# The low parts of the projection weights: formed on VectorE in place of GpSimd, with the steps of two recurrent branches ordered anew

## The chip, the cores and the metric

The kernel runs on one core of a Trainium2 chip. The metric is device time in microseconds (us) for one execution; of several runs the median counts. The engines are written as in the profile: PE is TensorE's matmul, PEld its weight load, DVE is VectorE, ACT is ScalarE, POOL is GpSimd, SP is SyncE, which issues most DMAs.

## The reference

One layer works on 512 tokens of width 1024 in float32. Cut to what matters here:

```python
h = _rmsnorm(x, norm1[l])
proj = h @ w_in[l]                      # 1024 -> 10256 columns
a_q, a_k, a_v, a_beta, a_alpha, a_gate, b_f, b_i, b_q, b_gate, g_a, g_b = _split_cols(proj)
...                                     # causal conv + silu on a_q, a_k, a_v
o_a = _gated_delta_rule(qa, ka, va, beta, log_alpha)        # 8 heads of 128
...
o_b = _hgrn2_recurrence(qb, 1.0 - f_gate, ib, jnp.log(f_gate))   # 8 heads of 128
y_a = ... @ w_branch_a[l];  y_b = ... @ w_branch_b[l]
x = x + (sigmoid(g_a) * y_a + sigmoid(g_b) * y_b) @ w_out[l]
x = x + _peer(_rmsnorm(x, norm2[l]), w_pq[l], ...)          # expert retrieval
return _rmsnorm(x, final_norm)
```

## The kernel before

**Weights come in units.** A unit is 128 columns of a weight matrix, held as 128 partitions x 1024 float32 (512 KB). The first 64 units of the projection are eight for each head (a_k, a_q, b_q, a_v, b_f, b_i, b_gate, a_gate); the gate units g_a and g_b are mixed in. `NPROJ` is 78: units 0 to 77 are worked off in the projection stage, which is the subject here; 78 and 79, then the branch matrices and all that follows belong to later stages.

**Each product is made of three.** `w_split` (L482) splits a unit: ACT copies `wraw` into `whi`, a rounded fp32r copy, and another engine forms the low part `wlo` = `wraw` - `whi` (L491). The activations h are split the same way into `hhi` and `hlo`. For each of eight slices of 128 rows `piece` (L503) issues three 128x512 matmuls: whi on hhi, wlo on hhi, whi on hlo; so a unit is 24 matmuls.

**Three buffers each.** The tiles wraw, whi and wlo have three buffers. When unit n begins, the projections load unit n+3 (`w_raw`, an SP DMA) and split unit n+2 (`w_cut`), so a split is due two units ahead of its use.

**The start.** For units 0 to 4 the matmuls run on unscaled h; meanwhile the token scales are found (ACT squares, DVE adds them into `acc`, PE sums across partitions, POOL takes the power, DVE spreads the scale into `rd`, PE broadcasts it). Then DVE scales these units' results and convolves a_k and a_q (L943, L947), then makes the scaled h slice by slice (L451) and splits it anew (`hlo`, L456, even slices on DVE, odd ones on POOL). Unit 5 needs that new split. `w_cut(2)` to `w_cut(6)` stand by hand between these steps.

**The rest of the stage is ordered by a planner.** Five generators run side by side: the set-up of gates and masks, branch A's state recurrence (`branch_a2`), branch A's preparation (`branch_a1`), branch B, and the projections. Each yields the tiles that its next step on PE reads. A class `Flow` keeps a model of every engine with a cost for every instruction and for the waits between engines. At each turn the loop takes the generator whose next step is ready first by that model, with small advantages (`BIAS`), and issues it. All engines then run their instructions strictly in the order in which they were issued. So a changed engine in one helper changes the costs, and with them the order of the steps on every engine. Branch A has a loop of 15 steps on POOL for each head (`xt`, `Xb`, L712 and L714) that inverts 16x16 blocks; its result goes out and back by DMA (L716 to L726) to `branch_a2`.

Of the kernel before, what the change touches and what calls it, by code (L numbers as in the profile page):

```python
# [51 lines left out]
NPROJ = 64 + 14  # L52
# [19 lines left out]
NDMA = 4  # L72
# [205 lines left out]
def build(ctx, tc, I, O):  # L278
# [6 lines left out]
    def act(o, i, f, **kw):  # L285
        nc.scalar.activation(o, i, f, **kw)  # L286

    vec, gps, pe = nc.vector, nc.gpsimd, nc.tensor
# [180 lines left out]
    N0 = len(order)  # L469
# [5 lines left out]
    raws, wts = {}, {}  # L475
# [6 lines left out]
    def w_split(raw, eng=gps):  # L482
        hi = wpool.tile([P, DC, UW], F32R, tag="whi", name="whi")
        lo = wpool.tile([P, DC, UW], F32R, tag="wlo", name="wlo")
        act(hi, raw, AF.Copy)
        if eng is None:

            act(lo, hi.bitcast(F32), AF.Copy, scale=-1.0)
            gps.dma_start(out=lo, in_=raw, accum_op=OP.add)
        else:  # L490
            eng.tensor_tensor(lo, raw, hi.bitcast(F32), OP.subtract)  # L491
        return hi, lo
# [5 lines left out]

    def w_cut(n):
        if n < len(order):  # L500
            wts[n] = w_split(raws.pop(n), vec if n < 2 else gps if n < N0 + NDMA else None)

    def piece(p, w, c, m):  # L503
        whi, wlo = w
# [8 lines left out]
    with ExitStack() as ph:  # L513
# [476 lines left out]
        def projections():  # L990
            def some():
                while late:
                    if next(late[0], True) is None:
                        return
                    late.pop(0)

            for n, (kind, h) in list(enumerate(order[:NPROJ]))[NF:]:
                while not allowed(kind, h):
                    some()
                    yield [None]  # L1000
                p = pst("mm", MMB)
                yield [wts[n][0], wts[n][1], p]
                w_raw(n + 3)
                w_cut(n + WB - 1)
                for c in range(DC):
                    piece(p, wts[n], c, hm)
                    some()
                    if n < NF + NTWO:
                        some()
                    if c < DC - 1:  # L1010
                        yield []
                wts.pop(n)
                late.append(consume(kind, h, p))
                if n >= NPROJ - 1:
                    while late:
                        some()
# [16 lines left out]
        for c in range(DC):  # L1033
            if c in (0, 2):
                cs = slice(2 * c, 2 * c + 4)
                act(wts[0][0][:, cs, :], raw[:, cs, :], AF.Copy)
                vec.tensor_tensor(wts[0][1][:, cs, :], raw[:, cs, :], wts[0][0][:, cs, :].bitcast(F32), OP.subtract)
            unscaled(xT, n1, c)
            piece(first[0], wts[0], c, hm)
            if c == W1:  # L1040
                w_cut(1)
        w_cut(2)
        w_raw(3)
        sums = pst("mA", 1)
        r = pst("mC", 1)
        rs = sbt("tmpB", 3)
        for k in range((NF - 1) * DC):
            n, c = 1 + k // DC, k % DC
# [566 lines left out]
    with ExitStack() as ph:  # L1615
# [132 lines left out]
        for i in range(-LEAD, P):  # L1748
            n = i + LEAD
# [66 lines left out]
```

## Time and profile before

| what | value |
|---|---|
| time, median of 3 runs (lowest, highest) | 2110.07 us (2106.29, 2113.62) |
| the profiled execution's own time | 2111.22 us |
| its span, first to last instruction | 2109.3 us |
| mean granted TensorE clock | 0.993 |
| busy in the span: PE, PEld, DVE, ACT, POOL | 97%, 83%, 69%, 44%, 55% |
| the stage under study | from the start to about 660 us of the span |

The shares are means over stages of very different kind; the second half of the program has DMA engines busy at 80% and more, the projection stage at 27%. What this change is worth has to be read in the first 660 us. A busy PE is a sum of modelled durations: matmuls overlap, so its share alone doesn't say that PE is at its rate.

### The profile page before, as it was taken

Reading aid. Unit: us, or ns where it says so; the run is one execution under the profiler, and the core shown is the slowest. Engines: PE = TensorE matmul, PEld = TensorE weight load, DVE = VectorE, ACT = ScalarE, POOL = GpSimd, SP = SyncE. Lnnn points to the kernel's source line nnn. Section 1 sums busy time; section 2 is a strip of 40 time slices with the busy share of each in tenths; the row PEclk is TensorE's granted clock in tenths of the full one; section 3 lists DMA queues with packets and bytes.
Section 4 is the critical chain, followed back from the end, with each engine's and each line's share of the span. In section 5 each row is a group of like instructions: output and inputs, shape, how many; then the busy total and the mean of one; then the engine's idle time right before and its main releaser. Section 6 shows DMA issues by size and latency. Waiting matters only on the chain. (4 is left out here: it accounts for less than half of the span.)

```text
span 2109.3 us, 34910 instructions
## 1 busy us (share of the span) xinstructions
PE 2039.1 (97%) x13210; PEld 1751.5 (83%) x13210; DVE 1450.8 (69%) x2779; ACT 936.4 (44%) x1742; POOL 1155.1 (55%) x957
## 2 busy tenths in 40 slices
PE   7899999999999999999899999999999999999997
PEld 5688787887878888888778999999999999999776
DVE  7666546656661375999995666676666667666897
ACT  5555555555554323666675333333333333333233
POOL 3565646654644644211002666676666666666887
PEclk9999999999999999999999999999999999999999
DMA  3322222132322644688799898988889888888785
GB/s 132 117 82 77 69 90 72 62 98 62 98 67 97 205 145 155 173 203 196 221 333 323 307 320 284 317 294 307 300 297 315 290 305 306 306 299 286 245 266 211
DMA packets 189463, 439.44 MB, mean 208 GB/s; under 512 B 26960, under 2 KB 90608, under 8 KB 187632
## 3 DMA queue, kind: packets, MB, share of 16 engines
q1 hardware_dynamic: 95248, 230.75, 32.2%
q0 software_dynamic: 42912, 156.26, 23.7%
q10 hardware_dynamic: 51136, 50.22, 7.2%
q8 instruction: 103, 1.69, 0.3%
q14 instruction: 64, 0.52, 0.1%
HBM read 375.81 MB, written 39.34 MB: 197 GB/s over the span
## 5 line engine op out<-in xcount | busy, mean ns | idle before, releaser
L491 POOL TENSOR_TENSOR wlo<-wraw,whi 128x1024 fp32r<-128x1024 f32 x204 | 501.1, 2457 | 290.5 <-ACT whi L286 283.1
L283 PE MATMUL h<-hhi,wlo 128*128 128x384 f32 x1024 | 347.0, 339 | 8.3 <-DMA wlo<-wraw 8.3
L283 PE MATMUL h<-hhi,whi 128*128 128x384 f32 x1024 | 347.7, 340 | 2.0 <-ACT hext L286 2.0
L283 PE MATMUL h<-hlo,whi 128*128 128x384 f32 x1024 | 346.7, 339 | 1.5 <-POOL hlo L456 1.1
L283 PE MATMUL mm<-hhi,whi 128*128 128x512 f32 x792 | 328.8, 415 | 1.0 <-ACT a_k L286 0.6
L283 PE MATMUL mm<-hlo,whi 128*128 128x512 f32 x792 | 311.5, 393 | 4.2 <-POOL hlo L456 3.0
L1707 DVE TENSOR_TENSOR wl<-hg,wh 128x384 fp32r<-128x384 f32 x126 | 129.4, 1027 | 269.5 <-ACT wh L286 269.5
L283 PE MATMUL mm<-hhi,wlo 128*128 128x512 f32 x792 | 309.6, 391 | 0.7 <-POOL wlo L491 0.7
L286 ACT ACTIVATE whi<-wraw 128x1024 fp32r<-128x1024 f32 (+1 forms) x251 | 263.6, 1050 | 103.1 <-PE mm L283 46.2
L283 PE MATMUL y<-vh,wl 128*128 128x512 f32 x756 | 298.7, 395 | 0.6 <-DVE wl L1707 0.6
L283 PE MATMUL y<-vl,wh 128*128 128x512 f32 x756 | 297.1, 393 | 0.9 <-POOL vl L1708 0.9
L283 PE MATMUL y<-vh,wh 128*128 128x512 f32 x756 | 295.1, 390 | 2.5 <-ACT wh L286 2.5
L1630 POOL DMA_INDIRECT row<-eu,eidx x128 | 158.3, 1236 | 145.9 <-DVE stage L1636 131.0
L1630 POOL DMA_INDIRECT row<-ev,eidx x128 | 160.9, 1257 | 126.5 <-DVE stage L1644 101.5
L286 ACT ACTIVATE hext<-h 128x384 f32<-128x384 f32 x88 | 43.1, 490 | 375.6 <-PE h L283 374.4
L283 PEld LDWEIGHTS h<-hhi,wlo 128*128 128x128 f32 x1024 | 193.7, 189 | 13.5 <-DMA wlo<-wraw 9.5
L283 PEld LDWEIGHTS h<-hhi,whi 128*128 128x128 f32 x1024 | 193.8, 189 | 6.6 <-ACT hext L286 2.6
L283 PEld LDWEIGHTS h<-hlo,whi 128*128 128x128 f32 x1024 | 193.7, 189 | 2.4 <-POOL hlo L456 1.8
L1644 DVE SCALAR_TENSOR_TENSOR stage<-row,stage 128x1024 f32<-128x1024 f32 x127 | 192.7, 1517 | 0.6
L1636 DVE CUSTOM_DVE_ANT_0 stage<-row,h2g 128x1024 f32<-128x1024 f32 x128 | 183.1, 1431 | 0.7
L283 PEld LDWEIGHTS mm<-hlo,whi 128*128 128x128 f32 x792 | 148.6, 188 | 40.1 <-POOL hlo L456 4.7
L283 PEld LDWEIGHTS mm<-hhi,whi 128*128 128x128 f32 x792 | 149.0, 188 | 27.6 <-ACT a_k L286 1.0
(431 smaller groups left out, 3675.2 us busy)
## 6 DMA issues: line engine op xcount, KB each, us to landing
wraw<-eut SPq DMA_DIRECT2D x128, 512.0 KB, 4.5
stage<-ev SPq DMA_DIRECT2D x126, 512.0 KB, 4.9
wraw<-wu SPq DMA_DIRECT2D x119, 512.0 KB, 4.1
stage<-gD ACTq DMA_DIRECT2D x31, 768.0 KB, 10.1
gD<-stage ACTq DMA_DIRECT2D x11, 2048.0 KB, 9.2
wlo<-wraw POOLq DMA_DIRECT2D x42, 512.0 KB, 5.7
sg<-sgD SPq DMA_DIRECT2D x16, 256.0 KB, 2.7
sgD<-tmpP SPq DMA_DIRECT2D x14, 256.0 KB, 2.1
```

The source lines that it names most:

```text
L283: nc.tensor.matmul(o, l, r, start=start, stop=stop)
L286: nc.scalar.activation(o, i, f, **kw)
L491: eng.tensor_tensor(lo, raw, hi.bitcast(F32), OP.subtract)
L1630: gps.indirect_dma_start(out=r, out_offset=None, in_=I["eu" if k < P else "ev"], in_offset=bass.IndirectOffsetOnAxis(ap=eidx[:, kk:kk + 1] ...
L1636: vec.tensor_tensor_reduce(out=junk, in0=r, in1=h2g, scale=1.0, scalar=0.0, op0=OP.mult, op1=OP.add, accum_out=hd[:, k:k + 1])
L1644: vec.scalar_tensor_tensor(yg, r, wgt[:, k - P:k - P + 1], yg, OP.mult, OP.add)
L1707: vec.tensor_tensor(wl, hg, wh.bitcast(F32), OP.subtract)
```

## The change

One expression differs. The engine that forms wlo is DVE for all units below 78, where it was DVE for units 0 and 1 only:

```diff
     def w_cut(n):
         if n < len(order):
-            wts[n] = w_split(raws.pop(n), vec if n < 2 else gps if n < N0 + NDMA else None)
+            wts[n] = w_split(raws.pop(n), vec if n < NPROJ else gps if n < N0 + NDMA else None)
```

So 76 subtractions of 128x1024 (units 2 to 77) go from POOL to DVE. The planner meets other costs and orders the stage anew; from the first unit of the next stage on, every engine's order is what it was.

The first place is DVE's queue during the start, while the first units are scaled and convolved; tmpA is a scaled unit, tmpP its convolution, rd the spread token scales.

```order
 L447 TENSOR_SCALAR rd<-ident,r_119 128x128 x4
 L980 TENSOR_TENSOR tmpA<-iv,tmpB 128x512
+L491 TENSOR_TENSOR wlo<-wraw,whi 128x1024
 L943 SCALAR_TENSOR_TENSOR tmpP<-a_k,convw,tmpP 128x511
 L943 SCALAR_TENSOR_TENSOR tmpP<-a_k,convw,tmpP 128x510
```

The low part of unit 4 now stands ahead of the first tap of a_k; those of units 2, 3, 5 and 6 are put between DVE's steps of the start in the same way.

The second place is DVE's queue in the first head's state recurrence, in the order of the change; P and XT are tiles that PE's next steps of branch A read, kn is branch A's normalized key of the next head.

```order
+L947 SCALAR_TENSOR_TENSOR a_k<-tmpP 128x512
+L742 TENSOR_TENSOR P_144<-iv,nbeta 64x256
+L491 TENSOR_TENSOR wlo<-wraw,whi 128x1024
+L756 COPY XT<-iv 64x4x64
+L646 TENSOR_TENSOR kn<-mA,rk 128x512
```

A low part now stands between the two DVE steps of the recurrence, and it waits for its whi from ACT; XT and kn are behind it.

The third place is PE's queue in the first head; mm are projections, pl<-z is a step of branch B, iv<-X,LT the first step of branch A's recurrence.

```order
 L283 MATMUL pl<-z 32x16 x16
-L283 MATMUL mm<-hhi,whi 128x512
-L283 MATMUL mm<-hhi,wlo 128x512
-L283 MATMUL mm<-hlo,whi 128x512
+L283 MATMUL iv<-X,LT 32x16 x16
 L283 MATMUL mm<-hhi,whi 128x512
 L283 MATMUL mm<-hhi,wlo 128x512
```

Branch A's recurrence of the first head is put next to branch B's steps, and so some projection matmuls come later. Counted over the whole stage, PE goes from branch work back to projection matmuls 198 times in the order before and 209 times in the new one; the matmuls are the same. The last branch step is followed by 105 matmuls on h before the next stage's first, where it was 48.

## Rows read from the trace of the kernel before

**Rows 1.** Busy time by stretch: the start, then the rest of the stage.
```profile
0.00:60.00 60.00, 45.63 (x179) 31.02 (x180) 43.31 (x70) 30.66 (x53) 22.76 (x23) 1.00 0.35 117
60.00:660.00 600.00, 587.87 (x5518) 479.17 (x5517) 356.81 (x603) 320.77 (x838) 340.84 (x442) 1.00 0.27 84
```
**Rows 2.** Timeline of PE at 38 us: start, duration, instruction.
```profile
37.88 0.39 PE L283 MATMUL mm<-hhi,whi 128*128 128x512 f32 x1
38.11 0.39 PE L283 MATMUL mm<-hhi,wlo 128*128 128x512 f32 x1
```
**Rows 3.** Waits of PE, 60 to 660 us: total, times, longest.
```profile
PE mA L563 <- ACT kT L286: 3.8, 4, 1.7
PE trb L625 <- DVE g L402: 1.8, 1, 1.8
PE mC L283 <- DVE SA L811: 1.4, 2, 0.8
PE mA L283 <- DVE AT L685: 1.2, 2, 0.8
PE iv L283 <- ACT XT L286: 1.0, 1, 1.0
```
**Rows 4.** Waits of PE, 0 to 60 us.
```profile
PE mC L283 <- DVE rd L447: 1.6, 1, 1.6
...
PE mA L283 <- DVE acc L433: 1.0, 1, 1.0
```
**Rows 5.** Groups by line, 0 to 700 us: busy, mean ns of one.
```profile
L283 PE MATMUL mm<-hhi,whi 128*128 128x512 f32 x608 | 256.5, 422 | 1.0 <-ACT a_k L286 0.6 <-ACT tmpP L286 0.4
...
L283 PE MATMUL mm<-hhi,wlo 128*128 128x512 f32 x608 | 237.8, 391 | 0.7 <-POOL wlo L491 0.7
```
**Rows 6.** Tile whi, 60 to 660 us: ns min/median/max; last row who waited.
```profile
L491 POOL TENSOR_TENSOR wlo<-wraw,whi x70: 2357/2381/2764, 60.1 to 652.6; 128x1024 fp32r<-128x1024 f32 x70
L286 ACT ACTIVATE whi<-wraw x70: 1039/1052/1115, 68.1 to 659.3; 128x1024 fp32r<-128x1024 f32 x70
...
  POOL wlo L491: 163.4, 43
```
**Rows 7.** Tile wlo, 0 to 30 us: unit 1's low part on DVE.
```profile
L491 DVE TENSOR_TENSOR wlo<-wraw,whi x1: 1226/1226/1226, 15.4 to 15.4; 128x1024 fp32r<-128x1024 f32 x1
```
**Rows 8.** Groups of DVE by form, 60 to 660 us.
```profile
L843 DVE TENSOR_TENSOR z<-b 128x512 f32<-128x512 f32 x56 | 46.9, 837 | 0.1
...
L943 DVE SCALAR_TENSOR_TENSOR tmpP<-a_v,convw,tmpP 128x511 f32<-128x511 f32 x8 | 14.2, 1772 | 9.5 <-ACT a_v L286 9.5
L953 DVE SCALAR_TENSOR_TENSOR a_gate<-a_gate,tmpP 128x512 f32<-128x512 f32 x8 | 13.5, 1689 | 8.3 <-ACT a_gate L286 8.3
...
L943 DVE SCALAR_TENSOR_TENSOR tmpP<-a_v,convw,tmpP 128x510 f32<-128x510 f32 x8 | 6.0, 748 | 0.2
...
L947 DVE SCALAR_TENSOR_TENSOR a_v<-tmpP 128x512 f32<-128x512 f32 x8 | 5.6, 695 | 3.8 <-ACT tmpP L286 3.6
```
**Rows 9.** Timeline of DVE, 14 to 76 us.
```profile
26.94 2.97 DVE L447 TENSOR_SCALAR rd<-ident,r 128x128 f32<-128x128 f32 x4
...
33.21 1.54 DVE L943 SCALAR_TENSOR_TENSOR tmpP<-a_k,convw,tmpP 128x511 f32<-128x511 f32 x2 [1.31 <-ACT a_k L286]
...
35.27 2.29 DVE L943 SCALAR_TENSOR_TENSOR tmpP<-a_k,convw,tmpP 128x509 f32<-128x509 f32 x1
...
41.82 3.53 DVE L451 SCALAR_TENSOR_TENSOR tmpP<-ogA,vecs,tmpB 128x512 f32<-128x512 f32 x2
```
**Rows 10.** Timeline of POOL, 14 to 76 us.
```profile
26.87 2.37 POOL L491 TENSOR_TENSOR wlo<-wraw,whi 128x1024 fp32r<-128x1024 f32 x1
```
**Rows 11.** Timeline of ACT, 14 to 76 us.
```profile
33.08 1.04 ACT L286 ACTIVATE whi<-wraw 128x1024 fp32r<-128x1024 f32 x1
...
41.09 1.04 ACT L286 ACTIVATE whi<-wraw 128x1024 fp32r<-128x1024 f32 x1
```
**Rows 12.** Timeline of DVE, 511 to 516 us.
```profile
512.31 2.15 DVE L953 SCALAR_TENSOR_TENSOR b_q<-b_q,tmpP 128x512 f32<-128x512 f32 x1
```

## Prediction

> **What bounds the kernel now.** I read the table of stretches first. From 60 to 660 us PE is busy 587.9 of 600 us, while DVE has 356.8, ACT 320.8 and POOL 340.8, at a full granted clock [rows 1]. So POOL, from which work is taken, is idle 43% of the stage, and DVE, which gets it, 41%. Since PE's busy time is modelled, I checked its rate in the timeline: where nothing disturbs them, projection matmuls start 0.23 us apart (37.88, 38.11), each shown as 0.39 long, so they overlap and PE goes from one straight into the next [rows 2]. The stage's length is PE's own work plus its gaps. The gaps are 600 - 587.9 = 12.1 us after 60 us, and 60 - 45.6 = 14.4 us before. The list of PE's waits says what ended them. After 60 us they are single events of 0.3 to 1.8 us, mostly for DVE and ACT; the five largest kinds make 9.2 us [rows 3]. Before 60 us the start chain counts: PE waits 1.0 us for the sums in acc and 1.6 us for rd [rows 4], and after that, slice by slice, for the new hhi and hlo.
>
> As the order of every engine is unchanged from the next stage on, the gain can be no more than what those gaps hold, and a loss can only come as new gaps or as more work of PE.
>
> **What the change removes.** 76 subtractions leave POOL. Of these, 70 lie after 60 us, with a median of 2.38 us [rows 6]: 70 x 2.38 = 167 us, half of POOL's busy time in the stage. PE doesn't wait for POOL there, so this alone is worth nothing. They also leave DVE's way. DVE instructions with everything in SBUF take far longer when they meet such a POOL instruction: the first tap of a convolution takes 1.772 us as a mean where the second of nearly the same size takes 0.748, a_gate's step 1.689 where a same-sized step takes 0.695, and the 56 z<-b take 0.837 [rows 8]. What is lost in the groups shown is 8 x (1.772 - 0.748) + 8 x (1.689 - 0.695) + 56 x (0.837 - 0.695) = 8.2 + 8.0 + 8.0 = 24 us; the two other convolutions and b_q behave as the ones shown, which makes some 45 us, as an estimate.
>
> The same is seen at the start, where rd's four 128x128 instructions take 2.97 us beside a POOL subtraction that began 0.07 us before them [rows 9, 10].
>
> **What it adds.** DVE does 76 subtractions. The trace has one of this form on DVE, unit 1's: 1.226 us [rows 7]. After 60 us that is 70 x 1.23 = 86 us. With 24 to 45 us of stalls gone, DVE's 357 us become 398 to 419, or 66 to 70% of 600. So DVE doesn't become the bound by its load.
>
> **The wait that comes with it.** The subtraction needs whi, a 1.05 us copy on ACT that is issued just ahead of it; POOL today waits 163 us at this place, 43 times [rows 6]. POOL could afford that; on DVE everything behind waits as well: the copies XT, the products P, LT, AT, kn and the states SA and SB that PE's next branch steps read. wlo also waits until PE has left the buffer of three units earlier. Its own reader is no worry: it is due two units, 48 matmuls or some 11 us, ahead of its use.
>
> **The sum, at the start.** The spreading of the scales: rd takes 2.97 us from 26.94 behind POOL's 26.87 to 29.24 [rows 9, 10]. In the new order unit 3's subtraction stands nine short instructions ahead on DVE; 1.2 us of it and some 0.6 us of rd end near 28.7 in place of 29.9, -1.2 us; with unit 2's no longer holding back the adds into acc I take -1.4, and PE's two waits [rows 4] would allow up to 2.6. Unit 4: DVE now waits for whi until 34.12 where it began a tap at 33.21 [rows 9, 11], and then works 1.2 us, +2.1; in return the tap at 35.27 loses its 1.5 us of stall: +0.6. Unit 5: whi is there at 42.13, the subtraction ends at 43.4, two scalings of some 0.7 us at 44.8, where they end at 45.35 today: -0.5. After that the slices go at DVE's and POOL's pace as before. Together -1.3 us.
>
> **The sum, from 60 us on.** Three of PE's gaps hang on a DVE instruction held by a POOL subtraction. The clearest is b_q's step at 512.31, 2.15 us long in place of 0.695 [rows 12]: XT and kT follow it, and PE waits some 1.6 us for kT, the longest of its four waits there [rows 3]. The others, by the timeline around them, are g (1.8 us) and XT (1.0 us) [rows 3]. With kT's 1.6 they hold 4.4 us; the order changes, so I take them as gone: -4.4. Then PE's own work: a projection matmul that follows branch work is longer. whi on hhi is always the first of its three and takes 256.5 us in all, wlo on hhi 237.8 [rows 5]; 18.7 us over 198 returns to the projections is 0.094 us each. The new order has 11 more: +1.0 us, and twice that if leaving costs as much; I take +1.5. Last, new gaps from waits for whi on DVE. From below nothing, since DVE has a third of its time free. From above 70 x 1.05 = 74 us, if each copy's whole length reached PE. The nearest row is what PE loses to all of DVE's 603 instructions today: trb, SA and AT, 4.4 us [rows 3]. 70 more instructions with a wait in front I put at half of that: +2.2.
>
> -1.3 - 4.4 + 1.5 + 2.2 = -2.0 us. The profiled execution took 2111.2, span 2109.3, and is 1.1 us above the median; from the median of 2110.1 the forecast is 2108.1 us. A measurement of this kernel tells about 0.3% or 6.3 us from no change, so this is "same", within 2104 to 2116.
>
> **The rivals.**
> - *The gaps close.* If with POOL out of its way DVE is never late, PE loses nearly all of the 12.1 us, keeps the -1.3 and pays 1.5: -11.9, 2098 us. For it: three of five kinds of gap trace back to held DVE work or a DVE queue. Against it: SA's and AT's don't show a subtraction in front, and a full, planned PE will have some gaps in any order. 0.20.
> - *DVE's queue stands at whi.* One place: a subtraction on DVE ahead of a step for PE, as with XT behind unit n's wlo in the order shown. ACT is behind its turn, DVE stands still, PE gets P, XT, SA or kn late and can't pass to other work, as its order is fixed. It decides at 0.15 us of new gap per unit: 70 x 0.15 = 10.5, against the other terms' -4.2, is the +6.3 that can be told. At 0.25 us, a quarter of a whi, it is +17.5 in place of +2.2: 2123 us. For it: the 163 us of waiting at this place [rows 6]. Against it: ACT is idle 47% of the stage, DVE too has slack, and few gaps of PE today end on DVE. 0.20.
> - *PE isn't the bound.* Then the branch chains set the length, and POOL's turns on them count: two or so subtractions stand in POOL's block loop of each head, 8 x 2 x 2.38 = 38 us, 2072 us. 0.03. The Trainium skill gives the reason to consider it (Perfetto Trace Analysis, Identifying the Most-Contended Engine): a matmul's busy share is no measure of distance to the limit, the weight loads' is. By that, 479 of 600 us [rows 1] leave a fifth of the stage open. The trace doesn't bear that out, since the matmuls follow each other at 0.23 us [rows 2].
> - *Nothing that can be told:* the forecast, 0.57.
>
> **How the numbers follow.** The gap-closing case and the third rival make "faster" 0.24 with a little of the forecast's edge; the standing queue makes "slower" 0.20; 0.56 remain. The forecast's own range is 2104 to 2115. The whole range reaches over the closed gaps down to 2097 and takes in the standing queue up to 0.2 us per unit, 2121; left out are the third rival and the ends of the other two, under 2 in 10.
>
> **What would show it.** In the profile after: 60 to 660 us with PE busy at 585 us or more; z<-b near 0.68 us and first taps near 0.75; DVE at 395 to 420 us, POOL near 175; wlo on DVE waiting for whi often, but PE's waits for XT, P, kn, SA and kT at 12 us or less in all; the start's last hlo 1 to 2 us earlier; more returns to the projections, each with a matmul of some 0.1 us more. Wrong would be a list of PE's waits with 20 us or more behind DVE tiles (the queue stands), or one that is nearly empty (the gaps closed). A time outside the range would mean that PE's rate in the stage isn't what I take it to be.

## The result, and the profile after

The change is slower: 2122.87 us (median of 6 runs, 2119.30 to 2125.99) against 2109.89 us before, a ratio of 1.0061 (95% interval 1.0046 to 1.0076). The forecast was 2108.1 us, in a range from 2097 to 2121. The profiled execution of the change is the fastest of the six, 2119.3 us with a span of 2117.5.

The first rows are PE's matmuls that open the next stage, from the timelines before and after: start, duration. All that the profile shows of the loss up to there is 702.24 - 695.96 = 6.3 us; the rest of the program takes 1415.3 us in place of 1413.3. The orders there are the same, and no run says where these 2.0 us come from.

```profile
695.96 0.39 PE L283 MATMUL mm<-ohi,whi 128*128 128x512 f32 x1
```
```profile
702.24 0.39 PE L283 MATMUL mm<-ohi,whi 128*128 128x512 f32 x1
```

Busy time by stretch after (answers to [rows 1]): PE, PEld, DVE, ACT, POOL, then the granted clock.

```profile
0.00:60.00 60.00, 46.90 (x183) 31.69 (x184) 45.40 (x79) 31.22 (x55) 10.51 (x18) 0.97 0.35 117
60.00:660.00 600.00, 580.26 (x5533) 471.05 (x5532) 365.82 (x675) 321.98 (x833) 191.50 (x369) 0.99 0.25 81
```

The start shows 1.3 us less of PE's gaps, but most of that is PE working longer at the lower clock of 0.97: in the run with X later (below), which has the same matmuls in the same order there at 1.00, PE is busy for 45.94 us. The 600 us behind the start have 19.7 us of gaps in place of 12.1. DVE's load has hardly grown and POOL's is down by 149 us, so no engine became the bound. PE's waits after (answers to [rows 3]) say where it stood:

```profile
PE iv L283 <- DMA X<-XD: 8.4, 5, 2.5
PE mA L283 <- DVE LT L672: 2.3, 3, 0.8
PE trb L625 <- DVE g L402: 1.7, 1, 1.7
PE pl L283 <- DVE z L848: 1.3, 3, 0.6
PE mA L563 <- DVE a_v L947: 0.9, 2, 0.6
```

The largest is new. PE stands at iv<-X,LT, the first step of branch A's recurrence, until the inverted blocks X are back from DRAM. Nothing of that size was in the list before: kT, at the head of it then, is gone, and X wasn't among the five largest.

DVE and POOL in the same 600 us (answers to [rows 6 to 8]): the groups by line, busy us and mean ns.

```profile
L491 DVE TENSOR_TENSOR wlo<-wraw,whi 128x1024 fp32r<-128x1024 f32 x68 | 92.1, 1354 | 32.0 <-ACT whi L286 31.9
L843 DVE TENSOR_TENSOR z<-b 128x512 f32<-128x512 f32 x56 | 38.4, 686 | 0.1
...
L943 DVE SCALAR_TENSOR_TENSOR tmpP<-a_v,convw,tmpP 128x511 f32<-128x511 f32 x8 | 6.1, 762 | 0.0
...
L953 DVE SCALAR_TENSOR_TENSOR a_gate<-a_gate,tmpP 128x512 f32<-128x512 f32 x8 | 5.5, 686 | 0.0
```

The stalls that POOL's subtractions gave DVE are gone: the first tap is at 0.762 us from 1.772, a_gate's step at 0.686 from 1.689, z<-b at 0.686 from 0.837. DVE waits 31.9 us for whi, a fifth of what POOL waited. By these rows the stalls went as the prediction says. So the question is whether the new order of the steps costs what was lost.

### The profile page after: what moved, and what is told of

Same layout as the page of the kernel before. It is cut to its first block, busy times and chain, and to the rows that moved or that the text cites. A ratio compares the mean times of both kernels' runs of the same rounds, so it can differ in the third digit from the quotient of the medians.

```text
span 2117.5 us, 34928 instructions
## 1 busy us (share of the span) xinstructions
PE 2040.3 (96%) x13210; PEld 1750.3 (83%) x13210; DVE 1466.6 (69%) x2855; ACT 939.8 (44%) x1742; POOL 995.6 (47%) x881
## 5 line engine op out<-in xcount | busy, mean ns | idle before, releaser
L491 POOL TENSOR_TENSOR wlo<-wraw,whi 128x1024 fp32r<-128x1024 f32 x128 | 319.9, 2499 | 101.5 <-ACT whi L286 99.9
```

## The experiments

All times are medians beside runs of the kernel before on the same chip (2109.97 to 2110.07 us), with the ratio to these.

**The engine and the order apart.** The planner can be told to cost one engine while the instruction is issued on another. That gives the two mixed cases. First, the low parts on DVE with the order of before:

```diff
 # Flow.note, after the instruction's engine is found
+            if e in ("DVE", "Pool") and ins.outs[0].bass_ap.tensor.name in self.planned:
+                e = self.planned[ins.outs[0].bass_ap.tensor.name]
...
 # w_cut
-            wts[n] = w_split(raws.pop(n), vec if n < 2 else gps if n < N0 + NDMA else None)
+            wts[n] = w_split(raws.pop(n), vec if n < NPROJ else gps if n < N0 + NDMA else None)
+            if 2 <= n < NPROJ:
+                flow.planned[wts[n][1].tensor.name] = "Pool"
```

> The low parts of units 2 to 77 on DVE as in the change, but the planner is told to cost them as POOL work, so every engine keeps the order of the kernel before. If the new order is to blame (branch A's recurrence issued before its inverted blocks are back, so that PE waits at iv<-X,LT), this is no slower than before: 2104 to 2110 us, with PE's waits for X under 1 us in all. If the engine is to blame (DVE's queue standing at whi, more work on DVE), it stays slow: 2118 to 2126 us.

Second, the low parts on POOL (`n < 2` as before, `"DVE"` told to the planner), with the order of the change:

> The low parts stay on POOL, but the planner is told to cost them as DVE work, so every engine has the order of the change. If the order is to blame, this is slower than the change itself, since POOL's block loop has the subtractions in it again while PE's order counts on its being short: 2130 us or more, PE's waits for X over 15 us. If the engine is to blame, it is near the kernel before: 2106 to 2114 us.

| low parts on | order of before | order of the change |
|---|---|---|
| POOL | 2109.97 | 2181.09, ratio 1.0330 (1.0316 to 1.0344) |
| DVE | 2104.65, ratio 0.9973 (0.9963 to 0.9983) | 2122.87, ratio 1.0061 (1.0046 to 1.0076) |

In the old order DVE is the better engine, by 5.3 us. The new order costs 18.2 us with the low parts on DVE, and 71 us with them on POOL. The sequence of every other instruction is the same in each column. So the loss is the order's. In the profiled executions the next stage starts at 689.72 us in the first mixed kernel and at 702.24 in the change, so 12.5 of the 18.2 us are seen up to there; PE's gaps from 60 to 660 us are 7.6 us in place of 19.7. That stretch, PE's waits in it and the low parts' wait for whi in the first mixed kernel (its lines are 3 to 5 numbers further on):

```profile
60.00:660.00 600.00, 592.43 (x5582) 483.91 (x5581) 362.76 (x678) 325.60 (x845) 185.36 (x371) 1.00 0.27 85
```
```profile
PE mC L286 <- DVE SA L816: 3.3, 3, 1.3
PE mA L568 <- ACT kT L289: 1.8, 2, 1.6
PE trb L630 <- DVE g L405: 1.0, 1, 1.0
```
```profile
L494 DVE TENSOR_TENSOR wlo<-wraw,whi x70: 1207/1226/2200, 68.3 to 651.9; 128x1024 fp32r<-128x1024 f32 x70
its engine sat idle before it (us, times) until:
  ACT whi L289: 50.5, 49
```

DVE stands 50.5 us at whi here, more than in the change, and PE's waits for SA grow from 1.4 to 3.3 us. In all three of them SA's step stands right behind a low part that waited for whi, as in the first:

```profile
185.18 1.23 DVE L494 TENSOR_TENSOR wlo<-wraw,whi 128x1024 fp32r<-128x1024 f32 x1 [3.45 <-ACT whi L289]
186.32 0.34 DVE L816 SCALAR_TENSOR_TENSOR SA<-SA,gl,mC 128x128 f32<-128x128 f32 x1
```

The second mixed kernel shows what the order asks for. Its waits of PE:

```profile
PE pl L286 <- DVE z L853: 27.4, 7, 8.1
PE iv L286 <- DMA X<-XD: 13.1, 5, 7.6
PE pl L286 <- DVE a L883: 5.6, 2, 2.8
```

The time came out as expected, the reason only in part: X is at 13.1 us, not over 15, and z is the largest. In the first head the block loop takes 13.7 us, less than in the change (16.4); it is late because it begins at 102.8 us in place of 87.4, as its first step Lb stands behind a subtraction on POOL. The longest wait comes from there by way of ACT. ACT's copy of the loop's result, XbT, stands in ACT's queue until the loop ends, and branch B's z, which PE needs, is behind it:

```profile
116.60 0.63 ACT L289 ACTIVATE XbT<-Xb 32x256 f32<-32x256 f32 x1 [10.18 <-POOL Xb L719]
117.13 0.70 ACT L289 ACTIVATE z<-z 128x256 f32<-128x256 f32 x2
```
```profile
118.47 0.74 PE L286 MATMUL pl<-z 128*32 128x16 f32 x16 [8.10 <-DVE z L853]
```

From 60 to 660 us ACT stands 57.7 us at XbT here, 19.1 in the change and 3.7 in the first mixed kernel.

**Only the start.** The kernel before with units 2 to 6 on DVE; the order is that of before.

```diff
-            wts[n] = w_split(raws.pop(n), vec if n < 2 else gps if n < N0 + NDMA else None)
+            wts[n] = w_split(raws.pop(n), vec if n < 7 else gps if n < N0 + NDMA else None)
```

> The kernel before with only units 2 to 6 moved to DVE; the order of all engines is that of before. By the prediction's sum the start ends 1.3 us earlier and nothing else changes: 2108 to 2109 us. If DVE's waits for whi at the start outweigh POOL's absence, it is 2111 us or more.

2108.91 us, ratio 0.9997 (0.9988 to 1.0006): the median moved by 1.1 us as summed, but the interval can't tell it from nothing. The trace can. POOL's last `hlo` of the start, before and in this kernel:

```profile
55.00 1.28 POOL L456 TENSOR_TENSOR hlo<-tmpP,hhi 128x512 fp32r<-128x512 f32 x1 [1.35 <-ACT hhi L286]
```
```profile
53.78 1.28 POOL L456 TENSOR_TENSOR hlo<-tmpP,hhi 128x512 fp32r<-128x512 f32 x1 [1.35 <-ACT hhi L286]
```

It begins 1.2 us earlier, where the sum said 1.3. The profiled execution doesn't keep that: its next stage starts at 696.11 us, against 695.96 before. The granted clock was 0.50 from 46 to 48 us and from 76 to 78 us, and 1.00 there in the kernel before.

**X later.** The change, with one arrival moved in the planner:

```diff
                 end = self.dma
+                if ins.outs[0].bass_ap.tensor.name.split("_")[0] in ("X", "XT"):
+                    end += 5000
```

> The change, with the planner told that the inverted blocks X and XT land 5 us later than it thinks; all its other numbers are the change's. If the waits at iv<-X,LT with what follows on them are the loss, it goes to 2105 to 2111 us and PE's waits for X to under 1 us. If the new order loses in other places too, it stays above 2114 us.

2116.26 us, ratio 1.0029 (1.0019 to 1.0039). It gains 6.6 of the 13 us by the medians. In the profiled executions it is 3.0, with the next stage at 699.16 us in place of 702.24. PE's gaps from 60 to 660 us are still 600 - 582.0 = 18.0 us, in place of 19.7, and the granted clock is 1.00 there. So the waits for X could be taken away and other waits came for them; the run doesn't show how much of the loss was X's, and the other places are real. PE's waits in it:

```profile
PE pl L285 <- DVE z L850: 4.4, 6, 1.1
PE iv L285 <- ACT XT L288: 3.0, 6, 0.8
PE poB L565 <- DVE tmpB L891: 2.8, 5, 1.6
```

X is no longer among them. In its place are many short waits for z and tmpB of branch B and XT of branch A. In PE's order of the change 272 of branch B's level matmuls (pl<-z) stand inside branch A's recurrences, 24 in the order before, 164 in this one.

**Branch A's recurrence only after branch B's levels.** This keeps the two branches apart; no cost is touched.

```diff
 # branch_a2
-                yield [X, XT, iv]
+                yield [X, XT, iv] + ([("BL", h)] if l == 4 else [])
...
 # branch_b, behind its loop over levels
+            res["BL", h] = idl
             eb = sbt("tmpB", 3)
```

> The change, with one more need for the planner: branch A's recurrence of a head may begin only after branch B's levels of the same head. No cost is altered. In the change's order 272 of branch B's level matmuls stand inside branch A's recurrences, in the order before 24, here none. If the new order loses because the recurrence is put there too early (waits for X, and two branches side by side that wait for the same DVE and ACT), both causes are gone: 2102 to 2108 us, PE's gaps from 60 to 660 us under 10 us. If only X's landing counted, it is near the run with X 5 us later, 2116 us; if the engine, 2122 us.

2111.97 us, ratio 1.0009 (1.0000 to 1.0018): 10.9 of the 13 us are back. No wait for X is left. It is some 4 us over what was expected and 7 us over the old order with the same engine. Its gaps after 60 us are 11.0 us; the expectation had under 10.

**The planner's cost of small POOL instructions.** In the traces a step of the block loop takes longer than the planner thinks: by the formula below, 180 ns and 2.15 ns for each element, a step of 45 elements, the mean of the loop, costs 277 ns, and in the change the two kinds of step take 478 and 451 ns. The change with 200 ns more on POOL instructions of under 256 elements:

```diff
-            return 180 + {"TensorCopy": 3.45, "TensorScalarPtr": 4.5, "Memset": 0.9}.get(op, 2.15) * n
+            return (180 if n >= 256 else 380) + {"TensorCopy": 3.45, "TensorScalarPtr": 4.5, "Memset": 0.9}.get(op, 2.15) * n
```

> The change, with one number of the planner altered: a POOL instruction of under 256 elements is costed 200 ns higher, near what the steps of the block loop take in the trace of the change. If the order is to blame, branch A's recurrence comes later on PE, the waits for X shrink from 8.4 us to under 3 us and the time to 2106 to 2114 us. If DVE's queue is to blame, nothing but chance moves it: 2118 to 2126 us.

2105.06 us, ratio 0.9977 (0.9968 to 0.9986): the whole loss is gone, with the low parts on DVE and only the order altered. Counted as above, 132 of branch B's level matmuls stand inside branch A's recurrences here, and the kernel is faster than the one with none: that they stand there is not by itself the loss. Its stretch after 60 us and its largest waits:

```profile
60.00:660.00 600.00, 594.26 (x5620) 482.79 (x5619) 364.81 (x681) 327.23 (x858) 187.39 (x376) 1.00 0.26 84
```
```profile
PE mA L283 <- DVE GT L626: 1.4, 1, 1.4
PE mA L283 <- DVE AT L685: 1.2, 2, 0.6
PE iv L283 <- ACT XT L286: 0.8, 1, 0.8
```

**Half of it, and more of it.** 280 and 480 in place of 380:

> The change with small POOL instructions costed 100 ns higher, half of the step that was tried. If the loss follows from how far the planned end of the block loop (30 instructions) lies ahead of the real one, the waits for X shrink only in part, to 2 to 5 us, and the time lies between: 2108 to 2117 us.

> The change with small POOL instructions costed 300 ns higher, beyond what the trace shows. Branch A's recurrence is then later than it need be, which costs nothing while PE has projections to do: no waits for X and 2102 to 2108 us. If lateness costs, it is slower than with 200 ns.

2107.85 us (0.9991, 0.9982 to 1.0000) and 2107.95 us (0.9989, 0.9980 to 0.9998). Half the step already takes the waits for X out of the list, so the expected middle way didn't show; all three values give an order better than the change's, and they differ among themselves by 3 us without a direction.

**The control.** The same 200 ns on the kernel before, low parts on POOL:

> The kernel before (low parts on POOL) with the planner's cost of small POOL instructions raised by the same 200 ns. It is the control: if that number is worth something only because the change made branch A's recurrence come too early, this stays within 0.3% of before, 2104 to 2114 us, since PE waits 0.4 us for X there. If the better cost is a gain of its own, whatever the engine of the low parts, it is 2105 us or less, and then the engine is not what made the corrected version fast.

2125.93 us, ratio 1.0074 (1.0060 to 1.0088). Neither side of the expectation had said so: the number that mends the change's order spoils the one of before, by 16 us. Its gaps from 60 to 660 us are 18.3 us, most at z (4.0) and at kT (3.6), with 0.7 us for X, and there are 4.3 us more up to 700 us, 3.9 of them at branch A's tmpA. So the better time of the corrected change isn't a better planner as such, and an order that the planner makes can be worse by 16 us for reasons other than X.

**Both corrections.**

> The same need together with small POOL instructions costed 200 ns higher. If the two corrections remove the same thing, it is no better than either alone, 2102 to 2108 us; if the cost also mends other places, some us less, 2099 to 2103 us.

2104.13 us, ratio 0.9973 (0.9962 to 0.9984): what the need removes, the corrected cost removes too, as the need adds only 0.9 us to it; the cost adds 7.8 us to the need. This, the corrected cost alone and the mixed kernel with the old order beat the kernel before by 5 to 6 us.

## Why the prediction was wrong

- **The bound was right.** The stage is PE's work plus PE's gaps. The prediction's last line, that a time outside the range would mean another rate of PE, is wrong: the projection matmuls still start 0.23 us apart (702.24, 702.47), and what is new are gaps: PE is busy for 580.3 us, where the prediction's sign asked for 585 or more. From 60 us to the next stage the gaps are 19.7 us after and 12.6 before, and the next stage starts 6.3 us later, with the start 1.7 us earlier by its last hlo. That accounts for 5.4 of the 6.3 us.
- **The start was right as far as the last hlo**: -1.3 summed, 1.2 us in the trace with only the start changed. That it reaches the time isn't shown.
- **DVE's relief was right in kind and undersized.** 24 to 45 us of stalls were summed. Measured: 92.1 us of new work raised DVE's busy time by 365.8 - 356.8 = 9.0, so some 83 us fell away. The sum left out two rows that also fell: z<-z,b_f from 596 to 428 ns and z<-z,b_q from 578 to 452, 56 times each, 16.5 us in all.
- **The wait for whi on DVE was put about right**: +2.2 us forecast; in the old order on DVE, SA's wait grew by 1.9 us, in the way that was forecast. The rival that DVE's queue stands at whi fell: it named the right sign and nearly the right time, but with 50.5 us of DVE standing there the kernel is faster than before.
- **The gaps from held DVE work were about right**: -4.4 forecast. With the old order on DVE, kT's waits fell from 3.8 to 1.8 us (the one behind b_q is gone; the longest was another, near 600 us, and is still 1.6 us), trb's from 1.8 to 1.0, and XT's is gone: -3.8. The three terms without the order's own give -1.3 - 4.4 + 2.2 = -3.5; the mixed kernel measured -5.3.
- **The step that failed is the one for new gaps**: "The nearest row is what PE loses to all of DVE's 603 instructions today". It bounded the new gaps by what DVE can hold back, as if the new order were the old one with other instructions in DVE's queue. The order's own price was put at 1.5 us, for 11 more returns to projections. Measured, it is 18.2 us with the low parts on DVE; what the 11 returns are of that wasn't measured apart. No rival had the new order in it. I showed the very row, iv<-X,LT put ahead of projection matmuls, and didn't ask whether X would be there by then.

What the order does is told by the rows around 104 us, the first head. SP issues and POOL's block loop in the change, then PE:

```profile
101.10 0.22 POOL L712 TENSOR_TENSOR xt<-Lb,Xb 32x28 f32<-32x28 f32 x1
101.40 1.28 POOL L714 TENSOR_TENSOR Xb<-Xb,xt 32x28 f32<-32x28 f32 x1
...
103.13 0.66 POOL L714 TENSOR_TENSOR Xb<-Xb,xt 32x15 f32<-32x15 f32 x1
```
```profile
103.81 0.33 SPq L716 DMA_DIRECT2D XD<-Xb  x1
...
105.55 0.39 SPq L725 DMA_DIRECT2D X<-XD  x1
```
```profile
106.54 0.89 PE L283 MATMUL pl<-z 128*32 128x16 f32 x32
109.90 0.89 PE L283 MATMUL iv<-X,LT 128*32 128x16 f32 x32 [2.47 <-DMA X<-XD]
```

The block loop ends at 103.8, its result goes out at 103.8 and comes back from 105.6 on; PE is done with its work ahead of that step at 107.4 and stands until 109.9. In all eight heads PE begins that step 2.8 to 5.0 us after X's way back is issued; in the order before it was 3.1 to 17.6. With the subtractions out of POOL's queue the planner counts on a short loop and puts branch A's recurrence there. By the trace the loop is shorter (16.4 us in the first head, 21.1 before), but not by so much as the costs of its steps say: they became longer, xt from 365 to 478 ns and Xb from 422 to 451 as a mean of 120:

```profile
L714 POOL TENSOR_TENSOR Xb<-Xb,xt 32x15 f32<-32x15 f32 (+7 forms) x120 | 50.7, 422 | 9.4
L712 POOL TENSOR_TENSOR xt<-Lb,Xb 32x15 f32<-32x15 f32 (+7 forms) x120 | 43.8, 365 | 7.8
```
```profile
L712 POOL TENSOR_TENSOR xt<-Lb,Xb 32x15 f32<-32x15 f32 (+7 forms) x120 | 57.4, 478 | 9.4
L714 POOL TENSOR_TENSOR Xb<-Xb,xt 32x15 f32<-32x15 f32 (+7 forms) x120 | 54.1, 451 | 9.4
```

The first pair is of the kernel before, the second of the change, both from 60 to 660 us. One reason for the growth is seen at 101.40: a step of 28 elements takes 1.28 us, where the same form took 0.24 at 88.25, and DVE's low part runs from 101.36 for 1.22 us:

```profile
101.36 1.22 DVE L491 TENSOR_TENSOR wlo<-wraw,whi 128x1024 fp32r<-128x1024 f32 x1 [0.45 <-ACT whi L286]
```

So POOL got back a part of the stalls that DVE lost: at most 17 us, by which these 240 steps grew. The Trainium skill has it both ways round (SBUF — State Buffer, SBUF: two separate sides): DVE and GpSimd hold a shared port pair for a whole instruction, and whoever comes second is blocked; an instruction of DVE with two SBUF inputs counts against one of GpSimd that reads SBUF. The trace agrees, with these 1.28 us. A planner that charges only DVE for such meetings, as `Flow.shared` does, misses this direction.

**What is shown and what stays open.** That the order is the cause is shown by the two mixed kernels. That branch A's recurrence comes too early in it is seen in the trace, with 8.4 us of waits for X where there were none. How much of the 18.2 us that is, the altered plans don't show, since each of them moves other steps too: 6.6 us return when X alone is planned later, 10.9 when the recurrence is kept behind branch B's levels, and the control shows that an altered cost can by itself make an order 16 us worse.

A second place is likely and not shown: ACT at XbT, as in the second mixed kernel. Planning X or the recurrence later leaves the planner's costs of the block loop as they were, and ACT still stands there 16.3 and 14.5 us, against 19.1 in the change. With the cost at 280 it is 1.7 us, and with 380, 480 or both corrections nothing. Among the kernels with the low parts on DVE, those that stand long there are the slow ones (2112 to 2123 us) and the others take 2104 to 2108; but no run moved XbT alone, and the kernel before stands there for 14.2 us at 2110. Why 380 ns gives a good order with the low parts on DVE and a bad one with them on POOL wasn't tried further and stays open.

## What to carry to other kernels

Where a planner sets the order, a changed engine is two changes, and they are measured apart by telling the planner the one thing and issuing the other: here -5 us for the engine and +18 us for the order. When PE is full and its order fixed, look in the new order for the first step of each chain, and ask of each of its inputs, DMAs included, when the trace says it arrives; the count of matmuls tells nothing about that. And a cost number that repairs one plan is no better model by that; run it on the other plan as well.

## What the runs showed of the hardware

The granted TensorE clock fell behind the two longest waits for X. The stretches of 2 us around the wait for X at 107.4 to 109.9 us in the change (PE, PEld, DVE, ACT, POOL, clock):

```profile
108.00:110.00 2.00, 0.10 (x3) 0.10 (x4) 1.91 (x3) 1.03 (x3) 0.00 (x0) 1.00 0.86 220
110.00:112.00 2.00, 2.00 (x52) 1.56 (x54) 1.46 (x5) 0.72 (x2) 0.00 (x0) 1.00 1.00 382
112.00:114.00 2.00, 2.00 (x27) 1.73 (x23) 0.92 (x3) 0.37 (x2) 0.00 (x0) 0.53 0.68 277
114.00:116.00 2.00, 2.00 (x7) 1.57 (x6) 0.76 (x2) 0.35 (x2) 0.00 (x0) 0.62 0.05 16
116.00:118.00 2.00, 2.00 (x67) 1.56 (x66) 0.00 (x0) 0.00 (x0) 0.00 (x0) 1.00 0.00 0
```

PE stood for 2.5 us, worked on at full clock for some 2 us, and then had 0.53 and 0.62, near the lower of its two levels, 1.2 GHz, while it was busy all the time. Its projection matmuls started 0.43 us apart there (113.62, 114.05, 114.48) in place of 0.23, so this gap cost twice. The same came behind the wait of 2.29 us, with 0.50 at 260 to 262 us, and not behind the one of 1.52 us:

```profile
258.15 0.79 PE L283 MATMUL iv<-X,LT 128*32 128x16 f32 x29 [2.29 <-DMA X<-XD]
181.31 0.79 PE L283 MATMUL iv<-X,LT 128*32 128x16 f32 x29 [1.52 <-DMA X<-XD]
```
```profile
260.00:262.00 2.00, 2.00 (x6) 1.61 (x6) 1.39 (x4) 0.72 (x2) 0.00 (x0) 0.50 0.68 277
182.00:184.00 2.00, 2.00 (x60) 1.56 (x57) 1.46 (x6) 0.72 (x2) 0.00 (x0) 1.00 0.84 264
```

The length of a gap doesn't decide it alone. At the start PE waits 2.02 us for hhi in the change, until 43.55, and has a clock of 0.59 from 44 to 48 us; with X later it waits 2.05 us at the same place and keeps 1.00. In the second mixed kernel, where PE stands for 57 of the 600 us from 60 us on, the mean there is 0.94, so a part of its 71 us is the clock's. The mean clock of the change's six runs is 0.987 to 0.991, and the slowest run has the lowest; but three runs have 0.991, the fastest with 2119.3 us among them, and the others took 2120.1 and 2123.2. So the clock may be part of why the median lost 13 us where the profile lost 8, and no run measured that by itself.
